# Recurrence gates as 64-row products, with sigmoids, exponentials and pooling sums queued anew, in a hybrid decoder layer

## The chip, the cores and the metric

The kernel runs on one core of a Trainium2 chip. The metric is the device time of one execution in microseconds (us). TensorE is called PE below, its weight loads PEld, VectorE DVE, ScalarE ACT, GpSimd POOL; SP is the engine whose queue starts most DMA transfers. Each engine works through its own queue in order; what one needs of another it waits for.

## The reference, cut to what matters

One layer, 1024 tokens, 1024 channels, float32. The part that matters is the mixer:

```python
z = rms_norm(h, norm_mix_g)
proj = z @ w_in                                   # 1024 -> 512 pool + 512 lru + 512 gate
# pooling: four groups of 128 channels, trailing windows w = 2, 4, 8, 16
d[g] = (sum of the last w values of u_pool[g]) / min(t + 1, w) - u_pool[g]
y_pool[g] = (d[g] @ pool_w[g] + pool_b[g]) * pool_scale[g]
# recurrence: 8 heads of 64 channels
u = causal_conv4(u_lru, conv_w, conv_b)
r = sigmoid(u[head] @ gate_a_w[head] + gate_a_b); i = sigmoid(u[head] @ gate_x_w[head] + gate_x_b)
log_a = 8 * r * log_sigmoid(lru_L); a = exp(log_a)
h_t = a_t * h_(t-1) + sqrt(1 - a_t^2) * i_t * u_t
y_lru = h_t * gelu(u_gate)
h = h + concat(y_pool, y_lru) @ w_out
# then a squared-ReLU MLP (1024 -> 4096 -> 1024), a gated per-layer embedding, a last RMSNorm
```

## The kernel before, in words

Channels lie on the 128 partitions, tokens along the free dimension. Every float32 operand of a product is split into a high part (a rounding copy on ACT, L152) and a low part (the difference, on DVE, L153), and every product is three matmuls: high x high, high x low, low x high (`mm`, L310). A matmul covers 128 rows (the contraction), 128 output channels and 512 tokens, so one 128 x 128 block against 1024 tokens is six matmuls.

The projections are called `wl` (the first three blocks, tile `ps_l`), then `project(0)` to `project(8)` with the weight tiles `wi0` to `wi8` and the outputs `ps_i0` to `ps_i8`: 8 blocks of six matmuls, 48 in all for each. `project(0)` is the last recurrence tile, 1 to 4 are the four pooling groups, 5 to 8 the gate branch. Weights come in two turns of buffers: the split of `wi5` can start once PE has finished with `wi3`. Outputs lie in PSUM, two tiles of 1024 tokens (`pp`) and four of 512 (`pd`), used in turn.

Around the projections DVE and ACT do the rest for the recurrence tiles o = 0..3 (two pairs) and the pooling groups g = 0..3. The names in the rows are these: `H[0..7]` print as `h`, `T[0..5]` as `t`, the operand pairs `B` as `y`.

- `conv`: normalise (L489), four taps, split.
- `lru_gates(pair)`, L516: per tile two products (gate a, gate x), sigmoids from PSUM (L526), then u times gate x (L527). The 64-channel heads lie two to a 128 x 128 block, with zeros off the diagonal: `tables` (L410) clears T[5] and loads the heads into it in eight transfers.
- `lru_scan(pair)`, L529: per tile Exp (L533), Tanh (L534), Square (L535) on ACT, a combination on DVE (L537); then Sqrt (L541), a product (L543) and the recurrence as a scan (L544). Sigmoid, Exp with Tanh, Sqrt and Gelu lie in different tables of ACT: a change costs an ACT_TABLE_LOAD.
- `pool_windows(g)`, L553: the windowed sum by doubling, log2(w) additions over 1024 tokens, then division by the count and the difference (L564 to L567), split.
- `pool_mix(pair)`, L571: a 128 x 128 product per group, evicted on DVE (L578), split again.
- `gate_out(o)`, L546: normalise, Gelu (L549), times the recurrence's output (L550), split.

The order in the queues isn't the order in the code. A scheduler of the language sets it from dependencies, the code's order and its own costs; only what `pin` marks, or `issue_after` names, is held. After the mixer come the output projection (`ps_o`), the MLP and the embedding, which the change doesn't touch.

Of the kernel before, what the change touches and what calls it, by code (L numbers as in the profile page):

```python
# [49 lines left out]
def block_kernel(  # L50
# [359 lines left out]
    def tables():  # L410

        one = ones_f[:, :16]
        tc.keep_in_program_order(
            nc.vector.tensor_tensor_scan(recip_t, one, one, 0.0, ALU.mult, ALU.add)
        )
# [5 lines left out]
        for pair in range(2):
            for a in range(2):
                for par in range(2):
                    r = slice(64 * par, 64 * par + 64)
# [81 lines left out]
    gate_w, mix_w = {}, {}  # L506

    def ask_gates(pair):
        gate_w[pair] = small_weights(f"gw{pair}", T[5][:, pair * HALF : (pair + 1) * HALF])

    def ask_mix():
        raw = wp.tile([P, S], F32, tag="raw", name="pw_raw")[:, :HALF]
        nc.sync.dma_start(raw, pool_w)
        mix_w[0] = small_weights("pw", raw)

    def lru_gates(pair):  # L516

        hi, lo = gate_w[pair]
        for t in range(2):
            o = 2 * pair + t  # L520
            ct, rt, _ = LSETS[t]
            for a, (dst, b) in enumerate(((rt, "ga_b"), (ct, "gx_b"))):
                ps = psum(f"ps_g{a}{o}")
                mm(ps, kblk(hi, 2 * a + t), kblk(lo, 2 * a + t), *B[4 + o], True, True)
                for hs, part in ps:
                    nc.scalar.activation(dst[:, hs], part, AF.Sigmoid, bias=col(b, o))  # L526
            nc.vector.tensor_tensor(H[o], H[o], ct, ALU.mult)  # L527

    def lru_scan(pair):  # L529
# [23 lines left out]
    def pool_windows(g, ps):  # L553
# [4 lines left out]
        cur, step, n = u, 1, 0  # L558
        while step < w:
            nxt = st[n % 2]  # L560
            nc.vector.tensor_tensor(nxt[:, step:], cur[:, step:], cur[:, : S - step], ALU.add)
            nc.vector.tensor_copy(nxt[:, :step], cur[:, :step])
            cur, step, n = nxt, 2 * step, n + 1
# [550 lines left out]
```

## Time and profile before

| | us |
|---|---|
| median of 3 runs (977.18 to 978.17) | 977.25 |
| the profiled execution | 977.54 |
| its span | 975.5 |
| PE busy | 964.8 (99%) |
| DVE busy | 757.0 (78%) |
| ACT busy | 442.7 (45%) |

The profiled execution took 2.0 us more than its span, and 0.3 us more than the median. A busy share is an average over stages; which engine sets the pace is read from each stage's rows.

### The profile page before, as it was taken

How to read it: one execution, taken by the hardware profiler on the slowest of the kernel's cores; microseconds unless marked ns; L12 is line 12 of the kernel's file. 1: busy time of each engine (PE TensorE's matmuls, PEld its weight loads, DVE VectorE, ACT ScalarE, POOL GpSimd, SP SyncE). 2: the span in 40 equal slices, each digit the busy share in tenths (PEclk: the TensorE clock that was granted, in tenths of full speed). 3: DMA queues.
4: the chain of work that ended last, by engine and by line, in shares of the span. 5: the costliest groups of instructions: out<-in, count | busy, mean ns of one | idle time of the engine just before them, and what ended most of it. 6: DMA issues, size and time to landing. Idle time of an engine off the chain costs nothing.

```text
span 975.5 us, 11507 instructions
## 1 busy us (share of the span) xinstructions
PE 964.8 (99%) x4472; PEld 805.2 (83%) x4472; DVE 757.0 (78%) x885; ACT 442.7 (45%) x528; POOL 99.1 (10%) x72
## 2 busy tenths in 40 slices
PE   9999999999999999999999999999999999999996
PEld 7888888888788888888888888888888888888996
DVE  7999995449887777677777899879775669784976
ACT  7377643336543343334333544444343337552534
POOL 0000000002523322332331000000000000000210
PEclk9999999999999999999999999999999999999999
DMA  6301243110245345434533897356532341031122
GB/s 231 105 23 33 87 151 107 45 43 30 82 152 201 119 140 177 159 119 160 196 119 137 307 368 254 110 194 202 174 118 90 108 151 44 3 127 44 44 87 87
DMA packets 46198, 125.04 MB, mean 128 GB/s; under 512 B 5312, under 2 KB 7360, under 8 KB 46144
## 3 DMA queue, kind: packets, MB, share of 16 engines
q1 hardware_dynamic: 46000, 124.27, 36.9%
q8 instruction: 35, 0.57, 0.2%
q14 instruction: 19, 0.16, 0.1%
q10 hardware_dynamic: 144, 0.04, 0.0%
HBM read 90.74 MB, written 33.55 MB: 127 GB/s over the span
## 4 chain that ended last, share of the span: by engine, by line
PE 95%; DVE 3%; ACT 1%; DMA 1%; issue 0%; SPq 0%; DVEq 0%
PE ps_P_u L320 31%; PE ps_P_d L320 31%; PE ps_i L320 10%; PE ps_o L320 9%; PE ps_e L320 8%; PE ps_l L320 3%; PE ps_g L320 1%; PE ps_j L320 1%; PE ps_p L320 1%; DVE h L968 1%; DMA h<-in_xT 1%; DVE a L153 1%; DVE a L156 0%; DVE t L984 0%; DVE wu_lo L153 0%
## 5 line engine op out<-in xcount | busy, mean ns | idle before, releaser
L320 PE MATMUL ps_P_d<-a,wd_P_hi 128*128 128x512 f32 x880 | 271.1, 389 | 0.0
L320 PEld LDWEIGHTS ps_P_d<-a,wd_P_hi 128*128 128x128 f32 x880 | 165.2, 188 | 34.4
L320 PE MATMUL ps_P_d<-a,wd_P_lo 128*128 128x512 f32 x440 | 171.3, 389 | 0.0
L320 PE MATMUL ps_P_u<-a,wu_hi 128*128 128x512 f32 x512 | 157.7, 389 | 0.0
L320 PE MATMUL ps_P_u<-y,wu_hi 128*128 128x512 f32 x384 | 118.1, 389 | 0.0
L320 PEld LDWEIGHTS ps_P_u<-a,wu_hi 128*128 128x128 f32 x512 | 96.1, 188 | 19.9
L659 DVE TENSOR_TENSOR t<-t,ps_P_u 128x512 f32<-128x512 f32 (+1 forms) x80 | 62.6, 784 | 47.9 <-PE ps_P_u L320 47.7
L320 PE MATMUL ps_P_u<-a,wu_lo 128*128 128x512 f32 x256 | 99.6, 389 | 0.0
L320 PEld LDWEIGHTS ps_P_d<-a,wd_P_lo 128*128 128x128 f32 x440 | 82.6, 188 | 17.4 <-DVE wd_P_lo L153 0.3
L320 PEld LDWEIGHTS ps_P_u<-y,wu_hi 128*128 128x128 f32 x384 | 72.1, 188 | 14.9
L320 PE MATMUL ps_i<-a,wi_hi 128*128 128x512 f32 x288 | 77.1, 389 | 0.0
L320 PE MATMUL ps_P_u<-y,wu_lo 128*128 128x512 f32 x192 | 74.8, 390 | 0.4 <-DVE wu_lo L153 0.4
L153 DVE TENSOR_TENSOR a<-wd,a 128x1024 fp32r<-128x1024 f32 x56 | 67.1, 1219 | 5.2 <-ACT a L152 4.1
L152 ACT ACTIVATE a<-wd 128x1024 fp32r<-128x1024 f32 x56 | 58.8, 1057 | 21.2 <-PE ps_P_d L320 10.2
L320 PE MATMUL ps_o<-y,wo_hi 128*128 128x512 f32 x256 | 68.4, 389 | 0.0
L320 PEld LDWEIGHTS ps_i<-a,wi_hi 128*128 128x128 f32 x288 | 54.1, 188 | 11.2
L152 ACT ACTIVATE wu_hi<-wu 128x1024 fp32r<-128x1024 f32 x24 | 25.5, 1062 | 78.3 <-PE ps_P_u L320 43.9
L152 ACT ACTIVATE wu_hi<-wu_raw 128x1024 fp32r<-128x1024 f32 (+1 forms) x25 | 25.3, 1011 | 78.2 <-PE ps_P_u L320 44.8
L320 PEld LDWEIGHTS ps_P_u<-a,wu_lo 128*128 128x128 f32 x256 | 48.0, 188 | 10.0
L320 PEld LDWEIGHTS ps_o<-y,wo_hi 128*128 128x128 f32 x256 | 48.0, 188 | 10.0
L152 ACT ACTIVATE wd_P_hi<-wd 128x1024 fp32r<-128x1024 f32 x24 | 25.4, 1060 | 58.2 <-PE ps_P_d L320 58.0
L153 POOL TENSOR_TENSOR wg_lo<-wg_raw,wg_hi 128x1024 fp32r<-128x1024 f32 x4 | 9.9, 2478 | 408.7 <-DVE h L953 382.1
(224 smaller groups left out, 1634.2 us busy)
## 6 DMA issues: line engine op xcount, KB each, us to landing
wd<-act SPq DMA_DIRECT2D x56, 512.0 KB, 5.6
act<-t SPq DMA_DIRECT2D x32, 512.0 KB, 4.3
wu_raw<-in_w_up SPq DMA_DIRECT2D x16, 512.0 KB, 3.7
wu<-in_w_up SPq DMA_DIRECT2D x16, 512.0 KB, 4.6
act<-wu SPq DMA_DIRECT2D x16, 512.0 KB, 4.5
wd<-in_w_down SPq DMA_DIRECT2D x16, 512.0 KB, 6.2
h<-in_xT SPq DMA_DIRECT2D x15, 512.0 KB, 4.3
wg_raw<-in_w_gate SPq DMA_DIRECT2D x12, 512.0 KB, 3.3
```

Source lines behind the costliest of these rows:

```text
L152: pin(nc.scalar.activation(hi, src, AF.Copy))
L153: pin((eng or nc.vector).tensor_tensor(lo, src, f32(hi), ALU.subtract))
L320: ins = nc.tensor.matmul(ps, w, z[:, hs], start=first and z is zhi and w is whi, stop=last and w is wlo, skip_group_check=more,)
L659: (eng or nc.vector).tensor_tensor(to, to if y is None else y, x, ALU.add)
L968: nc.vector.scalar_tensor_tensor(hv, hv, col("g_fin", o), rfin[:, hs], ALU.mult, ALU.mult)
```

## The change

Four things change in the mixer. A gate product now takes the 64 rows of one head alone, and gives gate a and gate x of that head side by side as 128 output channels; the products of the two heads, on rows 0 to 63 and 64 to 127, are issued in turns into two PSUM tiles. `lru_gates` works on one tile o and stands behind another projection for each: behind 1, 2, 4 and 5. Each sigmoid is now over 64 partitions (gate x crosses to the other half), eight logical ones for a pair instead of four. The exponentials of a pair are held behind the last sigmoid of the pair's second tile, the sigmoids behind the newest weight split. The windows 4, 8 and 16 are summed by a scan (add the newest, subtract the oldest). The pooling eviction goes from DVE to ACT. Gates and pooling weights are loaded by two transfers behind the third x tile, without the clearing, and split at once.

```diff
-        tc.keep_in_program_order(nc.vector.memset(T[5], 0.0))
-        rv = T[5].rearrange("p (n a t c) -> p n a t c", n=2, a=2, t=2)
...
-                    nc.sync.dma_start(rv[r, pair, a, :, r], gates[pair, a, par])
+        nc.sync.dma_start(T[5][:, FIRST], gates)
+        nc.sync.dma_start(T[5][:, SECOND], pool_w)
...
+    HEADS = slice(0, 64), slice(64, P)
+    def ask_small():
+        split(T[5], *small)
+
+    def lru_gates(o):
+        hi, lo = hl(0), hl(2)
+        ct, rt, _ = LSETS[o % 2]
+        zhi, zlo = B[4 + o]
+        ps = [psum(f"ps_g{h}{o}") for h in range(2)]
...
+        for n, (w, z) in enumerate(((hi, zhi), (hi, zlo), (lo, zhi))):
+            for (at, x0), (_, x1) in zip(*halves):
+                for r, x in zip(HEADS, (x0, x1)):
+                    nc.tensor.matmul(
+                        x, w[r, o * P : (o + 1) * P], z[r, at : at + HALF], start=n == 0, stop=n == 2
+                    )
+
+        with tc.issue_after(newest[0]):
+            for dst, b, rows in ((rt, "ga_b", HEADS), (ct, "gx_b", HEADS[::-1])):
+                for h, r in enumerate(rows):
+                    for hs, part in ps[h]:
+                        last = nc.scalar.activation(dst[HEADS[h], hs], part[r], AF.Sigmoid, bias=col(b, o)[r])
+        nc.vector.tensor_tensor(H[o], H[o], ct, ALU.mult)
+        return last.ins
+
+    def lru_scan(pair, gates):
...
+            with tc.issue_after(gates):
+                nc.scalar.activation(a, r, AF.Exp, scale=cneg[:, o : o + 1])
+                nc.scalar.activation(r, r, AF.Tanh, scale=cpos[:, o : o + 1])
+                nc.scalar.activation(m, a, AF.Square)
...
+            nc.vector.tensor_tensor_scan(cur[:, :w], ones_f[:, :w], u[:, :w], 0.0, ALU.mult, ALU.add)
+            nc.vector.tensor_tensor_scan(
+                cur[:, w:], u[:, w:], u[:, : S - w], cur[:, w - 1 : w], ALU.add, ALU.subtract
+            )
...
-                nc.vector.tensor_scalar(
-                    T[5][:, hs], part, col("pool_b", g), col("pool_s", g), ALU.add, ALU.mult
+                nc.scalar.activation(
+                    T[5][:, hs], part, AF.Identity, bias=pool_bs[:, g : g + 1], scale=col("pool_s", g)
                 )
...
     pool_windows(0, project(1))
     lru_gates(0)
-    ask_gates(1)
     pool_windows(1, project(2))
+    last = lru_gates(1)
     ps = project(3)
     normed(T[0], ps)
-    lru_scan(0)
-    lru_gates(1)
-    ask_mix()
+    lru_scan(0, last)
+    pool_mix(0)
     pool_windows(2, None)
     ps = project(4)
-    pool_mix(0)
+    lru_gates(2)
     pool_windows(3, ps)
     gate_out(0, project(5))
-    lru_scan(1)
+    last = lru_gates(3)
+    lru_scan(1, last)
     gate_out(1, project(6))
```

Three places in the queues show what moved. The first is PE behind `project(1)`, the gate products of tile 0 (`ps_g00`, `ps_g10`); before, with 128 rows each, gate a's six stand ahead of gate x's, and tile 1 follows at once:

```order
L320 MATMUL ps_g00_0_609<-y8_121,hl1_136 128x512
L320 MATMUL ps_g00_512_610<-y8_121,hl1_136 128x512
L320 MATMUL ps_g00_0_609<-y9_122,hl1_136 128x512
L320 MATMUL ps_g00_512_610<-y9_122,hl1_136 128x512
L320 MATMUL ps_g00_0_609<-y8_121,hl1_136 128x512
L320 MATMUL ps_g00_512_610<-y8_121,hl1_136 128x512
L320 MATMUL ps_g10_619<-y8_121,hl1_136 128x512 x2
L320 MATMUL ps_g10_619<-y9_122,hl1_136 128x512 x2
L320 MATMUL ps_g10_619<-y8_121,hl1_136 128x512 x2
L320 MATMUL ps_g01_0_628<-y10_123,hl1_136 128x512
```

Now the two heads take turns, twelve matmuls of 64 rows, and `project(2)` follows them:

```order
L520 MATMUL ps_g00_0_603<-y8_121,hl0_135 128x512
L520 MATMUL ps_g10_605<-y8_121,hl0_135 128x512
L520 MATMUL ps_g00_512_604<-y8_121,hl0_135 128x512
L520 MATMUL ps_g10_605<-y8_121,hl0_135 128x512
L520 MATMUL ps_g00_0_603<-y9_122,hl0_135 128x512
L520 MATMUL ps_g10_605<-y9_122,hl0_135 128x512
L520 MATMUL ps_g00_512_604<-y9_122,hl0_135 128x512
L520 MATMUL ps_g10_605<-y9_122,hl0_135 128x512
L520 MATMUL ps_g00_0_603<-y8_121,hl1_136 128x512
L520 MATMUL ps_g10_605<-y8_121,hl1_136 128x512
L520 MATMUL ps_g00_512_604<-y8_121,hl1_136 128x512
L520 MATMUL ps_g10_605<-y8_121,hl1_136 128x512
```

So a tile has 12 matmuls before and now, and the place of tiles 1, 2 and 3 is behind projections 2, 4 and 5; PE's order is otherwise that of the code.

The second place is ACT and DVE between `project(2)` and the low part of `wi5`. On ACT, before, pair 0's sigmoids were over by `ps_g11`, and Exp, Tanh and Square (L533 to L535) of its first tile came next:

```order
L526 ACTIVATE h_67<-ps_g11_638,vecs_137 128x1024
L152 ACTIVATE hl1_136<-t_68 128x512
L533 ACT_TABLE_LOAD
L533 ACTIVATE h_67<-h_67,sp_427 128x1024
L152 ACTIVATE y0_113<-t_68 128x1024
L534 ACTIVATE h_67<-h_67,sp_427 128x1024
L535 ACTIVATE h_67<-h_67 128x1024
L533 ACTIVATE h_67<-t_68,sp_427 128x1024
L534 ACTIVATE t_68<-t_68,sp_427 128x1024
L152 ACTIVATE wi4_hi_717<-wi4_raw_716 128x1024
L535 ACTIVATE t_68<-h_67 128x1024
```

Now (L538 to L540 are Exp, Tanh, Square) tile 1's sigmoids and pooling group 1's split `y2` stand ahead of them:

```order
L528 ACTIVATE t_68<-ps_g01_690,vecs_137 64x1024
L528 ACTIVATE t_68<-ps_g11_512_692,vecs_137 64x512
L528 ACTIVATE h_67<-ps_g01_690,vecs_137 64x1024
L152 ACTIVATE y2_115<-t_68 128x1024
L528 ACTIVATE h_67<-ps_g11_0_691,vecs_137 64x512
L528 ACTIVATE h_67<-ps_g11_512_692,vecs_137 64x512
L538 ACT_TABLE_LOAD
L538 ACTIVATE h_67<-h_67,sp_420 128x1024
L538 ACTIVATE h_67<-t_68,sp_420 128x1024
L539 ACTIVATE h_67<-h_67,sp_420 128x1024
L540 ACTIVATE h_67<-h_67 128x1024
```

On DVE, before, `wi5_lo` stood three rows behind the second recurrence scan of pair 0 (L544), and pooling group 1's split `y3` between the two scans:

```order
L544 SCALAR_TENSOR_TENSOR h_67<-h_67 128x1024
L153 TENSOR_TENSOR y3_116<-t_68,y2_115 128x1024
L543 TENSOR_TENSOR t_68<-t_68,h_67 128x1024
L489 TENSOR_TENSOR t_68<-ps_i3_722,rstd_71 128x1024
L544 SCALAR_TENSOR_TENSOR h_67<-h_67,t_68 128x1024
L561 TENSOR_TENSOR t_68<-t_68 128x1023
L562 COPY t_68<-t_68 128x1
L153 TENSOR_TENSOR wi5_lo_843<-wi5_raw_841,wi5_hi_842 128x1024
```

Now the five rows L542, `ps_i3` (L485), L542 and the two scans of window 8 (L569, L570) are followed by these (L547 to L549: memset, product, recurrence scan; L573 to L575: the window's corrections):

```order
L547 MEMSET h_67 128x1
L573 TENSOR_TENSOR t_68<-t_68,recip_t_69 128x7
L575 SCALAR_TENSOR_TENSOR t_68<-t_68 128x1017
L548 TENSOR_TENSOR h_67<-h_67 128x1024
L547 MEMSET t_68 128x1
L574 TENSOR_TENSOR t_68<-t_68 128x7
L549 SCALAR_TENSOR_TENSOR h_67<-h_67 128x1024
L548 TENSOR_TENSOR t_68<-t_68,h_67 128x1024
L153 TENSOR_TENSOR y1_114<-t_68,y0_113 128x1024
L549 SCALAR_TENSOR_TENSOR h_67<-h_67,t_68 128x1024
L153 TENSOR_TENSOR y5_118<-t_68,y4_117 128x1024
L153 TENSOR_TENSOR wi5_lo_815<-wi5_raw_813,wi5_hi_814 128x1024
```

So `wi5_lo` is the seventeenth row from pair 0's first L542, and that row waits for the Square on ACT.

The third place is DVE ahead of `wi8_lo`. Before, between the rows of `ps_i6` and it, stood an eviction (L578) and a Gelu product (L550):

```order
L544 SCALAR_TENSOR_TENSOR h_67<-h_67,t_68 128x1024
L153 TENSOR_TENSOR wi7_lo_1012<-wi7_raw_1010,wi7_hi_1011 128x1024
L550 TENSOR_TENSOR t_68<-t_68,h_67 128x1024
L489 TENSOR_TENSOR t_68<-ps_i6_0_1016,rstd_71 128x512
L153 TENSOR_TENSOR y9_122<-t_68,y8_121 128x1024
L489 TENSOR_TENSOR t_68<-ps_i6_512_1017,rstd_71 128x512
L578 TENSOR_SCALAR t_68<-ps_p2_1072,vecs_137 128x1024
L550 TENSOR_TENSOR t_68<-t_68,h_67 128x1024
L153 TENSOR_TENSOR wi8_lo_1096<-wi8_raw_1094,wi8_hi_1095 128x1024
```

Now the whole of pair 1's recurrence stands there (L542, L547 to L549), with the Gelu product L555 in it:

```order
L485 TENSOR_TENSOR t_68<-ps_i6_0_1004,rstd_71 128x512
L485 TENSOR_TENSOR t_68<-ps_i6_512_1005,rstd_71 128x512
L542 SCALAR_TENSOR_TENSOR h_67<-h_67 128x1024
L542 SCALAR_TENSOR_TENSOR t_68<-t_68 128x1024
L547 MEMSET h_67 128x1
L548 TENSOR_TENSOR h_67<-h_67 128x1024
L547 MEMSET t_68 128x1
L549 SCALAR_TENSOR_TENSOR h_67<-h_67 128x1024
L548 TENSOR_TENSOR t_68<-t_68,h_67 128x1024
L555 TENSOR_TENSOR t_68<-t_68,h_67 128x1024
L549 SCALAR_TENSOR_TENSOR h_67<-h_67,t_68 128x1024
L153 TENSOR_TENSOR wi8_lo_1084<-wi8_raw_1082,wi8_hi_1083 128x1024
```

On ACT the rows that this waits for are, from the high part of `wi7` on: a table, Gelu, a table, tile 3's six sigmoids with the split `y8` among them, a table, Exp twice, Tanh, Square, Tanh, Square, a table, Sqrt.

## Rows read from the trace of the kernel before

**Rows 1.** The page: span, and PE's busy time.

```profile
span 975.5 us, 11507 instructions
...
PE 964.8 (99%) x4472; PEld 805.2 (83%) x4472; DVE 757.0 (78%) x885; ACT 442.7 (45%) x528; POOL 99.1 (10%) x72
```

**Rows 2.** The chain that ended last, mixer: start us, us, what.

```profile
40.77 21.76 PE ps_i L320 x96
...
89.73 5.44 PE ps_g L320 x24
...
106.05 2.72 PE ps_p L320 x12
```

**Rows 3.** Busy time by stretch: PE, PEld, DVE, ACT, POOL, granted clock, DMA.

```profile
62.00:95.00 33.00, 33.00 (x147) 27.32 (x146) 31.81 (x37) 27.96 (x30) 0.00 (x0) 1.00 0.12 40
...
110.00:155.00 45.00, 45.00 (x200) 37.28 (x199) 38.97 (x44) 17.64 (x18) 0.00 (x0) 1.00 0.35 117
```

**Rows 4.** DVE in order of time, the mixer: start us, us, instruction.

```profile
76.25 1.22 DVE L537 SCALAR_TENSOR_TENSOR h<-h 128x1024 f32<-128x1024 f32 x1
78.66 1.29 DVE L489 TENSOR_TENSOR t<-ps_i,rstd 128x512 f32<-128x512 f32 x2 [1.19 <-PE ps_i L320]
79.86 0.15 DVE L562 COPY t<-t 128x1 f32<-128x1 f32 x1
...
87.04 2.29 DVE L544 TENSOR_TENSOR_SCAN h<-h 128x1024 f32<-128x1024 f32 x1
89.25 1.20 DVE L153 TENSOR_TENSOR y<-t,y 128x1024 fp32r<-128x1024 f32 x1
...
96.01 1.21 DVE L153 TENSOR_TENSOR wi_lo<-wi_raw,wi_hi 128x1024 fp32r<-128x1024 f32 x1
...
138.39 1.22 DVE L153 TENSOR_TENSOR wi_lo<-wi_raw,wi_hi 128x1024 fp32r<-128x1024 f32 x1
```

**Rows 5.** The gate products' instructions: duration ns, first and last start.

```profile
L320 PEld LDWEIGHTS ps_g<-y,hl x48: 187/188/188, 62.1 to 94.6; 128*128 128x128 f32 x48
L320 PE MATMUL ps_g<-y,hl x48: 389/389/390, 62.4 to 94.8; 128*128 128x512 f32 x48
```

**Rows 6.** The chain again, near the end: products of 256 columns.

```profile
938.81 6.17 PE ps_e L320 x54
```

**Rows 7.** ACT in order of time: splits, table, sigmoids, Exp, Tanh, Square.

```profile
52.24 2.00 ACT L152 ACTIVATE y<-h 128x1024 fp32r<-128x1024 f32 x2
...
63.19 1.28 ACT L526 ACT_TABLE_LOAD   x1
64.49 2.27 ACT L526 ACTIVATE h<-ps_g,vecs 128x512 f32<-128x512 f32 x3
66.64 1.27 ACT L526 ACTIVATE t<-ps_g,vecs 128x512 f32<-128x512 f32 x2
...
71.70 1.16 ACT L533 ACTIVATE h<-h,sp 128x1024 f32<-128x1024 f32 x1
72.76 1.04 ACT L152 ACTIVATE y<-t 128x1024 fp32r<-128x1024 f32 x1
73.70 1.14 ACT L534 ACTIVATE h<-h,sp 128x1024 f32<-128x1024 f32 x1
74.74 1.04 ACT L535 ACTIVATE h<-h 128x1024 f32<-128x1024 f32 x1
```

**Rows 8.** PE in order of time: warm-up, first gates, a wait (in brackets) in the MLP.

```profile
1.31 4.64 PE L432 MATMUL ps_l<-ones 128*128 128x512 f32 x10 [1.31 <-DVE ones L338]
...
62.37 4.24 PE L320 MATMUL ps_g<-y,hl 128*128 128x512 f32 x18
...
254.28 0.50 PE L320 MATMUL ps_P_u<-y,wu_lo 128*128 128x512 f32 x1 [0.45 <-DVE wu_lo L153]
```

**Rows 9.** SP's queue at the start, in order of time.

```profile
6.19 0.91 SPq L435 DMA_DIRECT2D h<-in_xT  x2
11.84 0.33 SPq L167 DMA_DIRECT2D wl_raw<-in_w_lru  x1
...
18.77 6.05 SPq L425 DMA_DIRECT2D t<-in_gates  x8
```

**Rows 10.** DMA issues of the first 40 us: count, KB, us to landing.

```profile
h<-in_xT SPq DMA_DIRECT2D x7, 512.0 KB, 5.9
```

**Rows 11.** The chain at the start: PE from the second x tile on.

```profile
11.40 24.33 PE ps_l L320 x106
```

More of the change, by code (lines that the diff above doesn't have):

```diff
@@ L151, in split @@
         if g is None:
-            pin(nc.scalar.activation(hi, src, AF.Copy))
+            first = pin(nc.scalar.activation(hi, src, AF.Copy))
             pin((eng or nc.vector).tensor_tensor(lo, src, f32(hi), ALU.subtract))
         else:
-            pin(nc.scalar.activation(hi, src, AF.Identity, scale=g))
+            first = pin(nc.scalar.activation(hi, src, AF.Identity, scale=g))
             pin(nc.vector.scalar_tensor_tensor(lo, src, g, f32(hi), ALU.mult, ALU.subtract))
+        return first.ins
     def raw_tile(name):
@@ L167, in load_weights @@
         queue.dma_start(raw, src)
-        split(raw, hi, lo, eng=eng)
+        newest[:] = [split(raw, hi, lo, eng=eng)]
         return hi, lo
@@ L416, in tables @@
         nc.vector.reciprocal(recip_t, recip_t)
-        tc.keep_in_program_order(nc.vector.memset(T[5], 0.0))
-        rv = T[5].rearrange("p (n a t c) -> p n a t c", n=2, a=2, t=2)
[L421 to L424, printed above, removed]
-                    nc.sync.dma_start(rv[r, pair, a, :, r], gates[pair, a, par])
+        nc.sync.dma_start(T[5][:, FIRST], gates)
+        nc.sync.dma_start(T[5][:, SECOND], pool_w)
     norm = Norm("n0", T[0], T[1:3])
@@ L461, in block_kernel @@
     lv = vecs[:, c0 : c0 + NLRU]
-    neg, e, s, s2, poly, cpos, cneg = (sp[:, i] for i in range(7))
+    neg, e, s, s2, poly, cpos, cneg, pool_bs = (sp[:, i] for i in range(8))
     nc.vector.tensor_scalar_mul(neg, lv, -1.0)
@@ L477, in block_kernel @@
     nc.vector.tensor_scalar_mul(cneg, cpos, -1.0)
+    c_b, c_s = COLS["pool_b"], COLS["pool_s"]
+    nc.vector.tensor_tensor(pool_bs, vecs[:, c_b : c_b + NPOOL], vecs[:, c_s : c_s + NPOOL], ALU.mult)
     def project(i):
@@ L504, in block_kernel @@
     LSETS = ((H[4], H[5], H[6]), (H[7], T[3], T[4]))
[L506 to L529, printed above, removed]
+    HEADS = slice(0, 64), slice(64, P)
[6 more added lines that the diff above has]
+        ps = [psum(f"ps_g{h}{o}") for h in range(2)]
+        halves = [
+            [(hs.start + n, x[:, n : n + HALF]) for hs, x in parts for n in range(0, hs.stop - hs.start, HALF)]
+            for parts in ps
+        ]
+        for n, (w, z) in enumerate(((hi, zhi), (hi, zlo), (lo, zhi))):
[12 more added lines that the diff above has]
+    def lru_scan(pair, gates):
         for t in range(2):
@@ L532, in lru_scan @@
             a, r, m = LSETS[t]
-            nc.scalar.activation(a, r, AF.Exp, scale=cneg[:, o : o + 1])
-            nc.scalar.activation(r, r, AF.Tanh, scale=cpos[:, o : o + 1])
-            nc.scalar.activation(m, a, AF.Square)
+            with tc.issue_after(gates):
+                nc.scalar.activation(a, r, AF.Exp, scale=cneg[:, o : o + 1])
+                nc.scalar.activation(r, r, AF.Tanh, scale=cpos[:, o : o + 1])
+                nc.scalar.activation(m, a, AF.Square)
             nc.vector.scalar_tensor_tensor(m, m, 1.0, r, ALU.add, ALU.mult)
@@ L557, in pool_windows @@
             normed(u, ps)
[L558 to L563, printed above, removed]
+        cur = st[g % 2]
+        if w == 2:
+            nc.vector.tensor_tensor(cur[:, 1:], u[:, 1:], u[:, : S - 1], ALU.add)
+            nc.vector.tensor_copy(cur[:, :1], u[:, :1])
+        else:
+            nc.vector.tensor_tensor_scan(cur[:, :w], ones_f[:, :w], u[:, :w], 0.0, ALU.mult, ALU.add)
+            nc.vector.tensor_tensor_scan(
+                cur[:, w:], u[:, w:], u[:, : S - w], cur[:, w - 1 : w], ALU.add, ALU.subtract
+            )
         nc.vector.tensor_tensor(cur[:, : w - 1], cur[:, : w - 1], recip_t[:, : w - 1], ALU.mult)
@@ L571, in pool_mix @@
     def pool_mix(pair):
-        whi, wlo = mix_w[0]
+        whi, wlo = hl(1), hl(3)
         for t in range(2):
@@ L584, in block_kernel @@
     conv(1, ps_l[1])
-    ask_gates(0)
+    ask_small()
     conv(2, ps_l[2])
@@ L1079 @@
     )
-    gates = np.stack([np.asarray(g)[0].reshape(2, 2, 2, 64, 64) for g in (gate_a_w, gate_x_w)])
-    gates = gates.transpose(1, 0, 3, 4, 2, 5)
+    ga, gx = (np.asarray(g)[0].reshape(NLRU, 2, 64, 64) for g in (gate_a_w, gate_x_w))
+    gates = np.stack([np.stack([ga[:, 0], gx[:, 0]], 2), np.stack([gx[:, 1], ga[:, 1]], 2)])
+    gates = gates.transpose(0, 2, 1, 3, 4)
     wu = np.asarray(w_up)[0].reshape(NT // 2, 2, P, NPAIR, 2, P).transpose(3, 2, 4, 1, 0, 5)
@@ L1093 @@
         "pool_w": c(np.asarray(pool_w)[0].transpose(1, 0, 2)).reshape(P, NPOOL * P),
-        "gates": c(gates),
+        "gates": c(gates).reshape(P, NLRU * P),
         "w_out": tiles(np.asarray(w_out)[0]),
```

8 lines of the change are left out of this document (3 added, 5 removed).

## The prediction

> **What bounds the kernel now.** I read the page first: PE is busy 964.8 of a span of 975.5 us [rows 1], so only what shortens PE's work, or makes PE wait, can move the time. Then the chain that ended last, in the mixer: it lies on PE, group behind group, without a break. 96 matmuls take 21.76 us, 24 gate products 5.44, 12 pooling products 2.72, all 0.2267 us each [rows 2]. By stretch, PE is full (33.00 of 33, 45.00 of 45) at a granted clock of 1.00, so 2.4 GHz; but DVE is nearly full too between 62 and 95 us (31.81 of 33), and ACT has 27.96 [rows 3]. The room behind PE is thus small there, and the question is when weights and PSUM tiles are ready, not how busy an engine is.
>
> That room is read from DVE's queue. The low part of `wi5` begins at 96.01 [rows 4] and ends at 97.2; PE wants it only behind 12 pooling products from 106.05, so at 108.8 [rows 2]: 11 us to spare. The low part of `wi8` begins at 138.39 and ends at 139.6; PE comes to `project(8)` at 106.05 + 2.72 + 21.76 + 2.72 + 10.88 = 144.1 [rows 2]: 4.5 us to spare. What starts both chains is early: pair 0's first combination (L537) stands at 76.25 [rows 4].
>
> **PE's gain.** There are 48 gate matmuls before and now. If two of 64 rows run at once, they take 24 places of 0.2267 us: 48 x 0.2267 - 24 x 0.2267 = 5.44 us less, 1.36 for each tile.
>
> Two at once needs two weight loads in one place. A load of 128 rows takes 188 ns [rows 5], and two of those are longer than 227. But near the end, 54 matmuls of 256 columns take 6.17 us, 114 ns each, with a load each [rows 6]: loads can follow at 114 ns, two in 228. I take the full gain; the other bound is none of it, as before. The Trainium skill, TensorE: Matmul & The Clock Gate, section LDWEIGHTS, says that a load's time goes by its columns and not its rows, so halving the rows wouldn't shorten it. By that, with 188 ns for each load, a tile would take 2.26 us instead of 1.36; with the two stalls below shrinking in step, the sum would come out near 978.3 instead of 977.4. The row of 114 ns speaks for the smaller price.
>
> **What the new order makes late: wi5.** Durations overlap a little: a DVE operation over 1024 columns lasts 1.22 and the next begins 1.14 later, a scan 2.29 and 2.21 [rows 4]; on ACT a split holds the queue 0.95, a table load 1.30, a half sigmoid 0.60 (0.70 where nothing follows it), Exp 1.06, Tanh 1.04, Square 1.04 [rows 7]. The new pooling scan isn't in the trace; I price it as the recurrence's scan, which it resembles most (two operands, a running value); the other bound is an addition, 1.14.
>
> The first read of `ps_i2` was at 78.66, behind 24 gate matmuls less 6 that came after it; now 6 places stand there instead of 24, so 4.08 earlier: 74.58. From there, each row in its queue:
> - DVE, pooling group 1: two reads 1.21, a scan of 4 columns 0.1, `wi4_lo` 1.14, scan 2.21, corrections 0.07 + 1.14 + 0.15. Sum 6.02, to 80.60.
> - ACT, which has stood waiting for this with `y2` at its head: `y2` 0.95, two half sigmoids 0.60 + 0.70, table 1.30, Exp twice 2.12, Tanh 1.04, Square 1.04, hand-over 0.05. Sum 7.80, to 88.40.
> - DVE, which waited for the Square with nothing else to do: eight operations of 1.14 (9.12), three scans of 2.21 (6.63), five small ones 0.3, `wi5_lo` itself 1.22. Sum 17.27, to 105.67.
>
> PE in that time: 62.37 [rows 8] + gates 1.36 + `project(2)` 10.88 = 74.61; + gates 1.36, `project(3)` 10.88, pooling 2.72, `project(4)` 10.88, gates 1.36 = 101.81; four matmuls need the high part alone, 0.91: 102.72. **PE waits 3.0 us.** Part of it comes earlier, since `project(5)` takes the PSUM tile of the second pooling product, whose eviction stands in the same chain.
>
> **And wi8.** `project(5)` has 44 matmuls left at 105.7 and ends at 115.69; with its last high part, at 115.5, ACT can start `wi7_hi`. Then ACT without a gap: `wi7_hi` 1.06, table 1.30, Gelu 1.06, table 1.30, six sigmoids with `y8` 5.5, table 1.30, Exp, Exp, Tanh, Square, Tanh, Square 6.2, table 1.30, Sqrt 1.06, hand-overs 0.1. Sum 20.2, to 135.7. DVE behind the Sqrt: product 1.22, scan 2.21, product and Gelu product 2.28, scan 2.21, `wi8_lo` 1.22. Sum 9.14, to 144.84. PE from 115.69: gates 1.36, `project(6)` 10.88, pooling 2.72, `project(7)` 10.88, four matmuls 0.91: 142.44. **PE waits 2.4 us.** The second wait stays whatever the first is, since its chain begins where `project(5)` ends.
>
> The same sums over the queues of before give 96.0 and 138.2 for the two low parts, against rows of 96.01 and 138.39 [rows 4].
>
> **The rest.** A wait for weights costs a little more than its length: the one in the MLP is followed by a matmul of 0.50 instead of 0.39 [rows 8]; two make 0.2. Two more table loads, twice the sigmoids (18.2 us instead of 9.1, at 2.27 for three [rows 7]) and the evictions on ACT are in the chains above where they matter, and elsewhere under PE; the tail behind `project(8)` (read, Gelu, product, split) has the same four steps as before. The fewer additions on DVE are hidden as well. At the start, the two transfers go ahead of the x tiles: x tile 4 was issued with tile 3 from 6.19, and now follows `wl3`, issued at 11.84 [rows 9], so at 12.2; landing in 5.9 [rows 10] and split in 2.4, it is there at 20.5, and PE wants it at 11.40 [rows 11] + 3 x 4.08 = 23.6. Tile 5 at 15.0 lands at 20.9 and has `wl4` behind it on ACT and DVE: 23.1, again in time, with 0.5 to spare. The eight gate transfers that held SP for 6.05 us [rows 9] are gone. I put this at nothing, with 0.5 as its other bound.
>
> **Sum.** 977.54 - 5.44 + 3.0 + 2.4 + 0.2 = 977.7 for an execution like the profiled one, which is 0.3 above the median: **977.4 us**, no change. About 0.2% (2 us) is what a measurement of this kernel can tell from none.
>
> **Rivals.**
> - *The gain arrives*: the waits don't form, 977.25 - 5.44 = 971.8. Against it stand some 40 rows of known length in two queues. 6%.
> - *Half the gain arrives*: sigmoids over 64 partitions cost half (no row shows one): 0.65 less in the first chain, 2.3 in the second, 974.5. Or the pooling scan costs an addition: two of them in the first chain, 975.3. 14% together.
> - *The products don't pair*, which is the change not doing what it says: PE takes 1.36 more per tile, the chains start 1.36 later, and the waits shrink to 0.3 and 1.1: 0.2 + 0.3 + 1.1 over before, 978.8. 12%, still no change by the bound.
> - *Slower: the clock falls in the waits.* No row shows PE idle for 2 us once warm. The warm-up matmuls follow at (4.64 - 0.39) / 9 = 0.47 us [rows 8], the lower level of 1.2 GHz, over 4.6 us. The same behind each wait is ten matmuls at 0.24 more, 2.4 each: 982.1. It decides if even one wait does it (979.7). [...] The longest gap the trace has behind the start, 0.45 us, says nothing. 10%.
> - *Slower: the loads lie bare* between 64-row products: 48 x (0.19 + 0.23) = 19.9 us instead of 10.9, with no waits left: 986. 4%.
>
> **How the numbers follow.** The forecast has 54%, and its own spread is 975.5 to 979.3 (0.5 us for each hand-over chain, 0.5 for the start, the drain of PE between 128 and 64 rows, which is at most 389 - 227 = 0.16 us [rows 5] for each of eight changes, of which only the first two come ahead of the chains). Within 0.2%: 54% + 12%, less the tails, 0.62. Faster: 20%. Slower: clock, bare loads and the forecast's own tail, 18%. The range takes in the cheaper sigmoids and most of one lower clock: 974.2 to 981.0; the full gain and the two dearest cases stay outside.
>
> **What would show it.** PE idle for about 3 us near 102 to 106, released by ACT (an eviction) and then by DVE's `wi_lo`; and for 2.4 near 143, by `wi_lo`. DVE idle for 4 us before its first L542, waiting for L540. Gate products of one tile in 1.4 us, starts of two heads together. Wrong would be: no PE waits; 64-row sigmoids of other than 0.6 and 1.05 us; a granted clock under 1.00 behind the waits.

## The result, and the profile after

Measured beside each other on one chip, eleven executions each, the changed kernel takes 980.25 us and the kernel before 978.17 (medians). The ratio, which is taken from all executions, is 1.0026, its 95% interval 1.0017 to 1.0036. By it the change is 2.5 us slower, just over the 2 us that I called the bound of no change, and inside the range.

The profiled execution of after (980.25 us, span 978.5) shows both forecast waits. Of PE's timeline these rows carry the reading (start, duration, instructions, in brackets the idle time ahead and its releaser):

```profile
61.34 0.61 PE L318 MATMUL ps_i<-a,wi_lo 128*128 128x512 f32 x2
61.88 1.66 PE L520 MATMUL ps_g<-y,hl 64*128 64x512 f32 x12
63.47 1.20 PE L318 MATMUL ps_i<-a,wi_hi 128*128 128x512 f32 x4
64.50 0.62 PE L318 MATMUL ps_i<-a,wi_lo 128*128 128x512 f32 x2
...
100.86 1.66 PE L520 MATMUL ps_g<-y,hl 64*128 64x512 f32 x12
102.70 1.20 PE L318 MATMUL ps_i<-a,wi_hi 128*128 128x512 f32 x4 [0.18 <-ACT t L587]
105.85 0.73 PE L318 MATMUL ps_i<-a,wi_lo 128*128 128x512 f32 x2 [1.95 <-DVE wi_lo L153]
...
142.25 1.07 PE L318 MATMUL ps_i<-a,wi_hi 128*128 128x512 f32 x4
145.39 0.88 PE L318 MATMUL ps_i<-a,wi_lo 128*128 128x512 f32 x2 [2.07 <-DVE wi_lo L153]
146.07 1.91 PE L318 MATMUL ps_i<-a,wi_hi 128*128 128x512 f32 x4
147.77 1.05 PE L318 MATMUL ps_i<-a,wi_lo 128*128 128x512 f32 x2
148.63 1.36 PE L318 MATMUL ps_i<-a,wi_hi 128*128 128x512 f32 x4
149.83 0.62 PE L318 MATMUL ps_i<-a,wi_lo 128*128 128x512 f32 x2
...
157.08 1.07 PE L318 MATMUL ps_o<-y,wo_hi 128*128 128x512 f32 x4
```

The first four rows price a tile's gate products. They begin 0.54 behind the start of two matmuls that normally take 0.45, last 1.59 to the next start, and the four matmuls behind them take 1.03 instead of 0.91: 0.09 + 1.59 + 0.12 = 1.80 us, where before 12 matmuls took 2.72 [rows 2]. A view of 0.1 us of PE shows that the matmuls of the block start two together (duration in ns, first and last start):

```profile
L520 PE MATMUL ps_g<-y,hl x2: 493/493/493, 61.9 to 61.9; 64*128 64x512 f32 x2
```

By such views the pairs start at 61.88, 62.22, 62.45, 62.68, 62.92 and 63.14: 0.23 apart, but 0.34 behind the first pair, and 0.33 from the last to the next block.

The next two blocks hold the waits: PE idle at `project(5)` and at `project(8)`, each ended by the low part of that project's weights. Behind the second, 12 matmuls take from 145.39 to 149.83, 4.44 us instead of 2.72. The windows (busy time of PE, PEld, DVE, ACT, POOL; the clock; DMA) say the same by stretch; before, the clock was 1.00 in all three ([rows 3] has the outer two):

```profile
62.00:95.00 33.00, 33.00 (x155) 26.53 (x156) 26.80 (x31) 27.96 (x31) 0.00 (x0) 1.00 0.10 34
95.00:110.00 15.00, 12.87 (x61) 9.75 (x60) 15.00 (x16) 11.39 (x13) 0.00 (x0) 1.00 0.10 35
110.00:155.00 45.00, 42.93 (x187) 34.53 (x186) 31.22 (x29) 34.00 (x35) 0.00 (x0) 0.96 0.33 117
```

In the third window the granted clock falls to 0.96, so part of it ran at the lower of the two levels, 1.2 GHz (by windows of 1 us it is 0.50 from 146 to 149); in the second it stays at 1.00, though that holds the first wait. This is one execution: the mean granted clocks of the eleven go from 0.993 to 0.997, the profiled one's being 0.997, and those of 0.994 or less took 981.2 to 981.6 us, so some lost more to the clock than it.

The chain behind the first wait is DVE's timeline; `wi5_lo` stood at 96.01 before [rows 4]:

```profile
88.44 1.22 DVE L542 SCALAR_TENSOR_TENSOR h<-h 128x1024 f32<-128x1024 f32 x1 [4.27 <-ACT h L540]
...
92.05 2.33 DVE L570 TENSOR_TENSOR_SCAN t<-t 128x1016 f32<-128x1016 f32 x1
...
101.26 2.28 DVE L549 TENSOR_TENSOR_SCAN h<-h,t 128x1024 f32<-128x1024 f32 x1
103.46 1.20 DVE L153 TENSOR_TENSOR y<-t,y 128x1024 fp32r<-128x1024 f32 x1
104.58 1.22 DVE L153 TENSOR_TENSOR wi_lo<-wi_raw,wi_hi 128x1024 fp32r<-128x1024 f32 x1
```

DVE is idle for 4.27 us until the first Square, works without a gap to `wi5_lo`, and PE starts 0.05 after that ends. The first combination was forecast for 88.40.

**The budget.** I take the stretch from the first gate product to the first matmul of `ps_o`: 61.88 to 157.08, 95.20 us. Before, it went from 62.37 [rows 8] to this row, 92.47, so it is 2.73 longer now:

```profile
154.84 1.07 PE L320 MATMUL ps_o<-y,wo_hi 128*128 128x512 f32 x4
```

Gates: 4 x (2.72 - 1.80) = 3.68 less. First wait: 0.25 for the PSUM tile (102.70, where the gates of 100.86 + 1.59 were over at 102.45), 2.12 for the weights (105.85 less 102.70 + 1.03), 0.12 in the two matmuls behind. Second wait: 145.39 less 142.25 + 0.91, 2.23. Lower clock behind it: 4.44 - 2.72 = 1.72. Sum -3.68 + 2.49 + 2.23 + 1.72 = 2.76. The rest of the span gives 0.5 at the start and takes 0.8 in the MLP's second half (its down projection). Neither is the change's: in the profiles below, which share the changed start, the first gate product begins anywhere from 61.69 to 62.61, and that half of the MLP, which nothing touched, takes 304.6 to 306.1.

### The profile page after: what moved, and what is told of

Read it like the earlier page. It is cut to its first block, busy times and chain, and to the rows that moved or that the text cites. A ratio compares the mean times of both kernels' runs of the same rounds, so it can differ in the third digit from the quotient of the medians.

```text
span 978.5 us, 11498 instructions
## 1 busy us (share of the span) xinstructions
PE 963.3 (98%) x4472; PEld 800.9 (82%) x4472; DVE 746.1 (76%) x865; ACT 459.5 (47%) x546; POOL 98.5 (10%) x72
## 4 chain that ended last, share of the span: by engine, by line
PE 88%; DVE 6%; ACT 3%; DMA 1%; issue 1%; SPq 0%; DVEq 0%; ACTq 0%
PE ps_P_d L318 31%; PE ps_P_u L318 30%; PE ps_o L318 9%; PE ps_e L318 8%; PE ps_i L318 6%; PE ps_l L318 3%; PE ps_j L318 1%; DMA act<-t 1%; DVE h L549 1%; DVE h L977 1%; DMA h<-in_xT 0%; DVE t L570 0%; ACT h L538 0%; DVE a L153 0%; ACT h L528 0%
```

## The experiments

My theory after the result: PE pays for two weight splits that stand late in DVE's queue, the clock falls behind the longer wait, and the pairing is real but dearer than 1.36 a tile. Rivals: the waits come from ACT's longer work or from the scan, wherever the gates stand; the slow matmuls wait for operands and not for the clock; products of 64 rows are shorter by themselves. The kernel before ran at 976.6 to 978.2 us from chip to chip, so ratios are compared and not times. "Stretch" is the one of the budget (before 92.47).

| kernel | ratio to before (interval) | PE waits, us: project(5), project(8) | clock, 110 to 155 | stretch |
|---|---|---|---|---|
| changed | 1.0026 (1.0017 to 1.0036) | 0.18 + 1.95, 2.07 | 0.96 | 95.20 |
| e1_lo_on_pool | 1.0014 (1.0005 to 1.0023) | 2.35, 1.05 | 1.00 | 94.11 |
| e2_wait_filled | 1.0009 (1.0000 to 1.0018) | 0.18, none | 1.00 | 93.64 |
| e3_heads_apart | 1.0032 (1.0020 to 1.0044) | 0.50, 2.37 | 0.96 | 96.14 |
| e4_old_places | 1.0035 (1.0021 to 1.0049) | none; 4.4 at the gates and right behind | 1.00 | 96.20 |
| e5_pool2_late | 1.0023 (1.0011 to 1.0035) | 0.87, 0.38 + 2.72 | 0.96 | 94.76 |
| e6_both_moved | 0.9967 (0.9954 to 0.9979) | 0.88, none | 1.00 | 89.69 |
| e7_no_hold | 1.0028 (1.0018 to 1.0039) | none, 3.17 + 1.29 | 0.92 | |
| e8_doubling | 1.0058 (1.0044 to 1.0071) | none, 3.69 + 2.57 | 0.92 | 97.51 |
| e9_gelu_no_ask | 1.0016 (1.0007 to 1.0025) | 0.87, 2.97 | 0.92 | 95.82 |
| e10_moved_apart | 0.9984 (0.9975 to 0.9992) | none, none | 1.00 | 91.03 |
| e11_moved_t3 | 0.9963 (0.9951 to 0.9976) | none, none | 1.00 | 88.82 |
| e12_evict_dve | 1.0102 (1.0088 to 1.0116) | 4.86, 0.83 + 3.79 | 0.96 | |

(e7 and e12 put matmuls of `ps_o` ahead of the second wait's end, so they have no such stretch. Three clocks fell in other windows: e1 0.89 and e12 0.97 from 95 to 110, e4 0.95 from 62 to 95. Waits and clocks are those of one profiled execution each.)

**Take the two splits out of DVE's queue.**

```diff
-todo += [(load_weights, w_in[i], f"wi{i}", S, None) for i in range(9)]
+todo += [(load_weights, w_in[i], f"wi{i}", S, nc.gpsimd if i in (5, 8) else None) for i in range(9)]
```

> The changed kernel with the low parts of wi5 and wi8 alone computed on GpSimd instead of DVE; the queues of PE and ACT are the same. Theory (the new waits come from the place of these two subtractions in DVE's queue): wi5_lo starts when wi5_hi is done on ACT (96.0 instead of 104.6) and the first wait of 2.0 to 2.1 us goes. The second chain starts where project(5) ends and so comes earlier as well; wi8_hi itself is late on ACT, so that 0.5 to 1 us of the second wait stays. Total about 975.5 us (974.5 to 976.5), under both kernels. Rival A (the waits only hide others right behind them: the eviction of the second pooling product, or wi6): at most 1 us is gained, 979 to 980. Rival B (only the lower clock behind the second wait matters): the same as theory for the end, but with the granted clock of 110 to 155 back at 1.00 only if the second wait falls under 1 us.

A quarter of the gain came: 1.2 us by the ratios, whose intervals overlap, and not 4.75. At the second place the theory held (1.05 left), at the first rival A: `wi5_lo` was ready at 98.85, but PE then waited 2.35 for its PSUM tile, whose eviction on ACT stands behind the same DVE chain. That chain had become 2.2 us longer, and DVE's timeline shows where:

```profile
95.36 1.22 DVE L548 TENSOR_TENSOR h<-h 128x1024 f32<-128x1024 f32 x1
96.51 2.36 DVE L574 TENSOR_TENSOR t<-t 128x7 f32<-128x7 f32 x1
...
98.79 2.28 DVE L549 TENSOR_TENSOR_SCAN h<-h 128x1024 f32<-128x1024 f32 x1
```

An operation on 7 columns, 0.16 us elsewhere, lasted until GpSimd was done:

```profile
95.89 2.96 POOL L153 TENSOR_TENSOR wi_lo<-wi_raw,wi_hi 128x1024 fp32r<-128x1024 f32 x1 [95.44 <-ACT wi_hi L152]
```

The second one on GpSimd (142.87, 2.76) did the same to a scan on DVE: 4.47 us at 143.31, and 2.28 elsewhere.

**Keep PE busy in the waits.**

```diff
+        for n in range(5 if i in (5, 8) else 0):
+            for hs, part in ps:
+                for at in range(0, hs.stop - hs.start, HALF):
+                    nc.tensor.matmul(part[:, at : at + HALF], kblk(whi, 0), A[0][n % 2][:, hs.start + at : hs.start + at + HALF], start=True, stop=True, skip_group_check=True)
```

> The changed kernel with 10 matmuls of 512 columns more ahead of project(5) and of project(8): the first high-part products, done into a PSUM tile that project then starts anew, so that the output is unchanged. They need only what the first four matmuls need, and take 2.27 us, in the waits. Theory (a wait costs its length, and the second one also the fall of the clock behind it): the chains on DVE and ACT are untouched, PE is busy in the waits, the granted clock of 110 to 155 us goes back from 0.96 to 1.00 and the matmuls behind the second restart take 0.23 us instead of 0.47: 978.5 us, 1.7 less than the changed kernel. Rival (the matmuls behind the restart are slow because their operands come late, not because of the clock): no change, 980.2, or 0.3 more where the products outlast the wait.

As the theory had it: the ratio falls by 0.0017, 1.7 us (the two intervals just touch), and the stretch by 1.56. The queues of DVE and ACT are as they were; PE's timeline at `project(8)`:

```profile
142.81 2.43 PE L482 MATMUL ps_i<-a,wi_hi 128*128 128x512 f32 x10
145.08 1.07 PE L318 MATMUL ps_i<-a,wi_hi 128*128 128x512 f32 x4
145.98 0.70 PE L318 MATMUL ps_i<-a,wi_lo 128*128 128x512 f32 x2
146.53 1.08 PE L318 MATMUL ps_i<-a,wi_hi 128*128 128x512 f32 x4
```

The four matmuls that took 1.91 (at 146.07 in after) take 1.08 behind ten useless ones. So some 1.7 us of the change's 2.5 were the clock's, and twenty matmuls more, done in the waits, cost nothing that shows.

**Don't alternate the heads.**

```diff
-        for n, (w, z) in enumerate(((hi, zhi), (hi, zlo), (lo, zhi))):
-            for (at, x0), (_, x1) in zip(*halves):
-                for r, x in zip(HEADS, (x0, x1)):
+        for r, own in zip(HEADS, halves):
+            for n, (w, z) in enumerate(((hi, zhi), (hi, zlo), (lo, zhi))):
+                for at, x in own:
```

> The changed kernel with the six products of head 0 of a tile all ahead of those of head 1, so that no two neighbours lie in different rows. Theory (neighbours in different rows run at once): a tile's gate products take 12 x 0.2267 = 2.72 us or more instead of 1.59, visible in the row of ps_g. The chains then start about 1.1 later at each of them, and PE comes 1.1 later per tile, so that most of it shows in the total only for the tiles behind the waits or where a chain starts: 981 to 983 us. Rival (the products of 1.59 us aren't pairs, but simply shorter because they have 64 rows): 1.59 us as before, and 980.2.

```profile
62.61 2.23 PE L520 MATMUL ps_g<-y,hl 64*128 64x512 f32 x12
64.77 1.20 PE L318 MATMUL ps_i<-a,wi_hi 128*128 128x512 f32 x4
```

Neither: a tile takes 2.16 to the next start, between 1.59 and 2.72. Pairs are real, but products in other rows overlap in part even when six of one head stand ahead of the other's: by narrow views, eight of the twelve start between 63.18 and 63.99, 0.12 apart in the mean. That 64-row products are shorter by themselves is refuted by the next run, in which six of one head go with none of the other beside them and start 0.23 us apart, as 128-row ones do (63.99 to 65.15, six starts). Two of them:

```profile
L520 PE MATMUL ps_g<-y,hl x2: 386/388/390, 64.7 to 64.9; 64*128 64x512 f32 x2
```

The total shows less than 1 us of the 4 x 0.57 that PE loses (the stretch 0.94): the first wait absorbs 1.6, while the second is 0.3 longer.

**Put the gates back in their old places** (both tiles of a pair at once, behind `project(1)` and `project(3)`; `pool_mix(0)` again behind `project(4)`).

> The changed kernel with the gates back in the places of before: both tiles of pair 0 ahead of project(2), both of pair 1 behind project(3); the 64-row products, the pooling scan, the evictions on ACT, the merged transfers and the exponentials queued behind the sigmoids stay. In this order the second tile's products stand with head 0 ahead of head 1. Theory (what costs is the place of each tile's gates, which starts the recurrence's chain some 12 us later in the program): the chain starts earlier, wi5_lo and wi8_lo come in time, and the gain of the products arrives, less what the unpaired tiles cost: 974 to 976. Rival (the waits come from ACT's longer work, twice the sigmoids and two evictions, wherever the gates stand): a wait of 2 us or more remains and the total is 978 to 981.

The theory fell in part: the weights came in time, but PE stopped at the gates themselves, 4.4 us in all, and the time is the rival's. These are pair 0's; pair 1's are 1.59 and 0.81, by the same two releasers:

```profile
62.50 3.03 PE L520 MATMUL ps_g<-y,hl 64*128 64x512 f32 x18
66.13 1.65 PE L520 MATMUL ps_g<-y,hl 64*128 64x512 f32 x6 [0.60 <-DVE t L485]
69.18 0.87 PE L318 MATMUL ps_i<-a,wi_hi 128*128 128x512 f32 x2 [1.40 <-ACT h L528]
```

Two tiles need four PSUM outputs at once. Those come free when DVE has read the projection ahead (L485) and by ACT's sigmoids (L528), which are now twice as many; one over 64 partitions is hardly shorter than one over 128, by the groups of before and after (busy us, mean ns):

```profile
L526 ACT ACTIVATE h<-ps_g,vecs 128x512 f32<-128x512 f32 x4 | 2.5, 686 | 0.0
L528 ACT ACTIVATE h<-ps_g,vecs 64x512 f32<-64x512 f32 x12 | 7.7, 678 | 0.1
```

So half of these waits are ACT's longer work, as the rival had it, only not for the weights. Spreading the tiles does avoid a wait; it also starts the recurrence later.

**Undo one part each: the hold on the exponentials, the scan, the eviction on ACT.**

```diff
-            with tc.issue_after(gates):
-                nc.scalar.activation(a, r, AF.Exp, scale=cneg[:, o : o + 1])
-                nc.scalar.activation(r, r, AF.Tanh, scale=cpos[:, o : o + 1])
-                nc.scalar.activation(m, a, AF.Square)
+            nc.scalar.activation(a, r, AF.Exp, scale=cneg[:, o : o + 1])
+            nc.scalar.activation(r, r, AF.Tanh, scale=cpos[:, o : o + 1])
+            nc.scalar.activation(m, a, AF.Square)
```

> The changed kernel without the rule that queues Exp, Tanh and Square behind the sigmoids of the pair's second tile; the queues then put tile 0's three ahead of tile 1's sigmoids, with six more table loads of 1.28 us in all, and wi5_lo stands behind the first scan on DVE and not behind both. Theory (this rule makes pair 0's first scan late and so the first wait): the first wait goes, but the second chain has two more table loads and its wait grows from 2.1 to 4 or 5 us: 979 to 982, no gain in sum. Rival A (the rule costs nothing since the sigmoids set the chain): both waits as they are, 980. Rival B (the rule is the whole cause of both waits): no wait of over 1 us, 975 to 976.

The first wait went and the second grew to 4.5 us, with the sum unchanged (1.0028): the theory. On ACT the second chain then has the sequence Sqrt, table, Exp, Tanh, Square, table, Gelu, table, Sqrt ahead of `wi8_hi`.

Additions by doubling in place of the scan:

> The changed kernel with the pooling sums by doubling additions, as before, instead of a scan. Theory (the waits come from the places, the scan is hardly shorter than what it replaces: 2.3 us against 2 to 4 additions of 1.14 to 1.22): the two waits stay within 1 us of 2.1 each, and the total within 1.5 us of the changed kernel's 980.25. Rival (the scan with two operands is the slow part of the first chain): the first wait falls by over 1.5 us.

The theory missed. The first wait went, as the rival had it, but not for its reason: DVE's queue was made anew, with only two of the third group's additions ahead of `wi5_lo`; what was put off came back in the second chain, where ACT stood 3.57 us for the fourth group's split, and PE waited 6.3 us at `project(8)`. The scan, with the queues that come with it, is worth some 3 us.

Evictions on DVE by `tensor_scalar`, as before:

> The changed kernel with the pooling products evicted on DVE again, as before. Theory (the first chain is DVE's from the Square on, and two evictions of 1.2 us more lie in it ahead of wi5_lo, while ACT's chain gets 1.2 shorter in the second): the first wait grows by 1 to 2.5 us, the second shrinks by up to 1.2; total 0 to 2 us over the changed kernel. Rival (ACT's evictions are what made the waits): both waits shrink and the total falls by 1 us or more.

Right in sign for the first wait (2.7 longer, as the two evictions in DVE's queue are) and wrong for the second, which grew as well, to 0.83 + 3.79: 0.0076 or 7.4 us over the changed kernel. So two of the change's parts, scan and eviction, pay for themselves in its order.

**Move what stands ahead of `wi5_lo`.** The third pooling group is split by 104.66 in after (103.46 + 1.20) and needed only by the products at 128.65:

```diff
...
-    lru_scan(0, last)
+    _, scans = lru_scan(0, last)
     pool_mix(0)
-    pool_windows(2, None)
+    with tc.issue_after(scans):
+        pool_windows(2, None)
```

> The changed kernel with the third pooling group (3.9 us of DVE work, which stands between pair 0's combinations and its scans) held behind the pair's last scan on DVE. Theory (the first wait is made by what stands ahead of wi5_lo in DVE's queue, and this group is what can go): wi5_lo ends near 98.4 instead of 105.8; the eviction that frees project(5)'s PSUM tile comes some 0.4 later instead, so that PE waits 0.5 to 0.7 us there and not 2.1. The second chain starts where project(5) ends, so the second wait of 2.1 stays, with the lower clock behind it, and the total falls by about 1.5 to 2 us against the changed kernel, to about the time of before (ratio 0.9995 to 1.0015). Rival (the wait only goes to the next thing that is late, the PSUM tile): a wait of 2 us or more there and no gain, ratio 1.0026.

The first wait fell to 0.87 (forecast 0.5 to 0.7), and almost nothing came of it. PE reached `project(8)` earlier and `wi8_lo` was not earlier: PE restarted at 145.32 (145.39 in after). The pooling group's split, now late, stands ahead of the sigmoids on ACT (start 109.54 instead of 106.00), and from there to `wi8_hi` ACT has no gap of over 0.23 us (in after it stood 1.71 ahead of `wi7_hi`, until PE released it at 115.71):

```profile
107.16 1.06 ACT L152 ACTIVATE y<-t 128x1024 fp32r<-128x1024 f32 x1 [1.61 <-DVE t L575]
108.24 1.28 ACT L528 ACT_TABLE_LOAD   x1
109.54 4.92 ACT L528 ACTIVATE h<-ps_g,vecs 64x512 f32<-64x512 f32 x6
...
116.50 1.28 ACT L555 ACT_TABLE_LOAD   x1
118.01 1.06 ACT L555 ACTIVATE t<-t 128x1024 f32<-128x1024 f32 x1 [0.23 <-DVE t L485]
119.09 1.28 ACT L528 ACT_TABLE_LOAD   x1
...
140.31 1.04 ACT L152 ACTIVATE wi_hi<-wi_raw 128x1024 fp32r<-128x1024 f32 x1
```

The second chain was thus ACT's own, and the next run shortens it.

**And the second chain**: the first Gelu, with two table loads for it alone, behind pair 1's exponentials, and `wi8` asked for one project earlier.

```diff
...
-        whi, wlo = weights()
+        whi, wlo = weights() if i < 8 else asked.pop(0)
...
-    gate_out(0, project(5))
+    normed(T[0], project(5))
     last = lru_gates(3)
-    lru_scan(1, last)
-    gate_out(1, project(6))
+    squares, _ = lru_scan(1, last)
+    with tc.issue_after(squares):
+        gate_out(0, None)
+    ps = project(6)
+    ask()
+    gate_out(1, ps)
```

> As the run before, and for the second wait: the first gate_out's Gelu and split held behind pair 1's exponentials on ACT, and wi8 asked for one project earlier. Theory: ACT's chain behind project(5) loses a Gelu, two table loads and a split (4.7 us), wi8_lo is done near 136.5 where PE comes to project(8) near 140: no wait, no fall of the clock (granted clock 1.00 from 110 to 155), and the gain of the products arrives: 5 to 6 us under the changed kernel, 3 to 3.5 under before (ratio 0.9964 to 0.997). Rival A (only the first wait's price comes back, something else is late at project(8) or at ps_o): ratio about 1.000. Rival B (the tail: the Gelu results that come later hold up the projection behind, ps_o): the end is no better than in the run before.

This is the theory's number: 0.9967, 3.2 us under before and some 5.8 under the changed kernel. `project(8)` runs through at the upper clock, though `wi8_lo` ends 3.7 us later than I had worked out (at 140.21, by DVE's timeline: 139.01 + 1.20); PE comes to it at 141.67:

```profile
110.00:155.00 45.00, 45.00 (x204) 36.77 (x203) 34.31 (x33) 36.62 (x39) 0.00 (x0) 1.00 0.37 129
```

Without the early request, the place in the queues is lost again:

> The version with both moves (e6_both_moved) without its early request of wi8. It tells which of the two edits at the second place does the work. Theory (the place of wi8 in both queues counts, and not only ACT's shorter chain): wi8_lo stands behind the splits of the Gelu results on DVE and ends near 142 where PE wants it at 140.5: a wait of 1 to 2 us at project(8), 1.5 us or more over e6_both_moved. Rival (the shorter chain on ACT is all): no wait, the same time as e6_both_moved.

A wait of 2.97, longer than forecast, and a clock of 0.92: 4.8 us over e6_both_moved. So the early request is needed. The Gelu's move alone hardly shortens the wait (0.38 + 2.72 in e5_pool2_late); whether the request would do without it no run shows.

**The products again, where no wait hides them**: e6_both_moved with the heads apart, and with the second eviction in a tile of its own (`T[5 - 2 * t]`).

> The version with both moves, with the products of head 0 ahead of those of head 1 as in e3_heads_apart: the price of alternating them, where no wait hides it. Theory (2.16 us for a tile instead of 1.59, all on PE's path now): 4 x 0.57 = 2.3 us more than e6_both_moved, about 975.9, and still about 0.8 under before. Rival (a wait elsewhere takes up the difference, as in e3_heads_apart, where 0.8 of 2.3 showed): under 1 us more.

> The version with both moves, with the second pooling product of a pair evicted into another tile (T[3], which is free then), so that it needn't wait for the split of the first one on DVE. Theory (the 0.88 us that are left at project(5) are this eviction): PE's wait there goes, and no other of over 0.3 us comes: 972.5 to 973, 0.6 to 1.0 under e6_both_moved, ratio to before 0.9955 to 0.9962. Rival (wi5_lo, which now stands behind two more operations on DVE, is late instead): the same time as e6_both_moved.

Heads apart, the time rises by 0.0017 or 1.7 us (the intervals just touch) and not 2.3, since the 0.88 us of waiting vanish behind the longer gates. Both of these kernels leave PE without a wait, so that their stretches price the gates: heads apart, 92.47 - 91.03 = 1.44 less than before, by the rows 4 x (2.72 - 0.09 - 2.16 - 0.12) = 1.40; alternated, 92.47 - 88.82 = 3.65, by the rows 3.68. The ends of e11_moved_t3's stretch:

```profile
62.16 1.66 PE L520 MATMUL ps_g<-y,hl 64*128 64x512 f32 x12
...
150.98 1.07 PE L318 MATMUL ps_o<-y,wo_hi 128*128 128x512 f32 x4
```

Taking away the 0.88 shortens the stretch by 0.87; the times of e6 and e11 don't tell them apart (the intervals overlap). e11_moved_t3 has the shortest stretch, though not the shortest span (972.3 against 971.8), and both are faster than the kernel before and the changed one.

## Why the prediction was right, and where it wasn't

The frame held: the gain is real, two waits for `wi5_lo` and `wi8_lo` eat it, and they stand where they were forecast. PE restarted at 105.85 (forecast 105.67) and 145.39 (144.84). DVE's 4 us ahead of L542, the prices of the sigmoids and the scan, and a start worth nothing came as written. It was the sum that was 2.6 us short: it gave 0.16 over before, the budget 2.76. The range held that with some luck, since the errors have both signs: the gates 1.76 dearer, the waits 0.80 cheaper, their restarts 1.64 dearer. What came is nearest to the rival of the falling clock with one fall (979.7), and one of my own signs of being wrong, a granted clock under 1.00 behind a wait, showed. The terms:

- *PE's gain of 5.44.* Mis-sized: 3.68. The products do pair, which refutes two rivals (no pairs, bare loads), but a tile costs 1.80 and not 1.36. I had the drain between 128 and 64 rows in the spread, at 0.16 at most for each change; it is 0.44 a tile, 0.22 for each change: 0.09 and 0.12 outside the block, and inside it the longer steps behind its first and its last pair. The Trainium skill, TensorEngine Tiling (Array Packing), section Key Properties, says that changing the tiling mode drains TensorE; the longer steps at the block's two ends agree with that.
- *The waits of 3.0 and 2.4.* Measured 2.37 and 2.23. They are shorter because PE comes to them later, at 103.73 and 143.16 (forecast 102.72 and 142.44), mostly by the dearer gates.
- *"A wait for weights costs a little more than its length", 0.2.* This step failed: 0.12 behind the first, but 1.72 behind the second, where the clock fell. I gave that rival 10% because no row showed PE idle for 2 us, and took 0.45 us for the longest gap. The trace of before has more: a wait of 0.62 (`n_ps`, at 967.35), and PE idle from 968.05 to the end, where the granted clock is 0.57 from 972 to 973 and 0.50 behind. And waits of 2 to 3 us were my own forecast, so the sum should have had their restarts between 0.1 and 2.4 each. e2_wait_filled shows that it is the clock.
- *"The second wait stays whatever the first is, since its chain begins where `project(5)` ends."* In after the chain does begin there: PE released `wi7_hi` at 115.71 (forecast 115.5). But ACT had no more than the 1.71 us to spare in which it waited for that. In e5, with the first wait shortened, the chain began earlier, at ACT's sigmoids, PE's restart stayed where it was, and the wait grew to 3.1. In e7 and e8 it grew to 4.5 and 6.3, but there the queues changed with it.

What stays open: why the clock held behind 1.95 us of idling in one place and fell behind 2.07 in another, and in e4 behind 0.60 and 1.40 close together, wasn't tried by itself. Nor does every execution pay alike: the five of e3 have mean clocks from 0.995, the profiled one, to 0.998, where the kernel before has 0.997 to 0.998.

## What to carry to other kernels

A gain on the bounding engine has to be followed along the queues of the others: here 3.7 us of matmul time were lost to two weight splits that stood late in DVE's and ACT's order, and moving two things that nobody needed yet, and asking for one weight tile earlier, brought back all but 0.9 of it. When one wait is taken away, look where the next engine in the chain was idle: if it has no gap left, the wait only moves on. And a wait of a matmul engine is priced with the restart behind it, by a row or from both sides.

## What the runs showed of the hardware

- The lower clock comes after short waits. Behind single idle times of 0.50, 0.88, 1.05 and 1.95 us PE went on at its pace; behind 2.07, 2.35, 2.37, 2.72 and 2.97 four matmuls took 1.5 to 1.7 us instead of 0.91, until the clock rose again (in after from 149 to 150). Behind 3.17 in e7 the first four still took 1.03, and the next four 1.81 instead of 1.07 to the end of the last. Each is one profiled execution.
- A load of 64 rows takes as long as one of 128 (184 ns against 188 [rows 5]), and yet 12 products with a load each, 2.21 us of loads, go in 1.59 us: loads in different rows overlap.
- Two things with no row before came out as priced: an ACT operation over 64 partitions costs nearly as much as over 128 (678 ns and 686), and a DVE scan that adds and subtracts as the one that multiplies and adds (2.33 and 2.28).
- A GpSimd subtraction held up DVE twice in e1_lo_on_pool, by 2.2 us each: 7 columns took 2.36 instead of 0.16, a scan 4.47 instead of 2.28. The Trainium skill, SBUF — State Buffer, section Who interferes with whom, says that a DVE instruction with two SBUF inputs contends with a GpSimd one that reads SBUF; the rows agree.
